# A two-layer hybrid attention block on one NeuronCore: one first h from alternating chunks, dot products respread, stream order changed

## The chip, the cores and the metric

The kernel runs on 1 core of one Trainium2 chip, as a single launch. The metric is device time in microseconds (us), the median of 3 runs. TensorE multiplies matrices (PE, its weight loads PEld), VectorE (DVE), ScalarE (ACT) and GpSimd (POOL) do the elementwise work, SyncE (SP) issues most of the transfers from memory. "span" is the time from the first to the last instruction of one profiled execution.

## The reference, cut to what matters

512 latent and 256 context tokens of width 1024 pass through two layers. Each layer is a mixer and an MLP, and each of these is preceded by an RMS norm whose result is shifted and scaled by a conditioning vector:

```
sh1, sc1, g1, sh2, sc2, g2 = split(silu(c) @ ada_w[i] + ada_b[i], 6)      # the same for c_ctx
h = rms_norm(x, norm_mix[i]) * (1 + sc1) + sh1                            # latent; context with its own vector
x = x + g1 * mixer(h)                                                     # layer 0: window + neighbourhood, layer 1: latent attention
x = x + g2 * square(relu(modulate(rms_norm(x, norm_mlp[i]), sh2, sc2) @ w1)) @ w2
```

Layer 0's mixer projects h once (units kva, qa01, qa23, kqb0 to kqb3 and vb0 to vb3), runs 16 heads of attention in pairs, and projects the result. Layer 1's mixer is a low-rank latent attention.

## The kernel before, in words

Activations lie with the 1024 features on partitions, in 8 tiles k of 128 x 768 tokens (512 latent, 256 context). Nearly every product is made in three passes of TensorE: an operand is split into a high part and a remainder (hh and hl for h, wh and wl for weights), and `mm3` and `mm3t` add hh*wh, hl*wh and hh*wl. Weights arrive as 512 KB tiles through three buffers (`Weights`, `raws`); `pump` splits a tile (copy to wh, subtraction to wl on DVE or POOL) when a planner's clock says that it is near.

**The first stage** (from L1922) is written out by hand. Sixteen chunks of 512 KB of the conditioning matrix `ada_w` (scale: e = 1, shift: e = 0; four chunks c of 256 columns, two halves each) are issued by SP, all scale chunks first, with 1 KB rows. `part(e, c)` multiplies a chunk pair by the conditioning vectors, ACT copies the row out, and `turn(e, c)` transposes it and forms two tiles' worth of `mod` and, for the scale, of `coef`. Squares of x are taken by ACT and added by DVE (`acc`), `stats` sums them on PE, `rsq` gives 1/rms per token (`box`).

h is formed twice. `scaled(k)` makes hh and hl of x * coef, without 1/rms and without shift (2 ACT and 2 DVE operations per k), and `step(k)` adds tile k's part of the kva projection from them (18 matmuls, six outputs `first` in six PSUM banks). `hat(k)` multiplies x by 1/rms on POOL, and `whole(k)` applies scale and shift (2 ACT), copies hh (DVE or ACT) and subtracts hl (DVE or POOL). The missing shift of kva is made up by `shift_w` (24 matmuls on the split shift) and `shift_p`, and 1/rms and shift enter as `first` is copied out at the head of `mixer0`, by 12 DVE operations.

**The mixers** (`mixer0` L985, `mixer1` L1351) are ordered by `weave` (L233) while the program is built. Streams (projections `gemms`, `preps`, `finishes`, `scores` for the two halves of a head pair, `values`, the output projection's early part) yield what they wait for. A model of the engines (`Clock.note`, L67) estimates when each could go on (a transfer counts as its bytes / 350e3 us behind the one before, plus 2.0: 3.5 us for 512 KB); the earliest goes next, nothing counts as earlier than 0.4 us after PE's modelled time, and among equals the first in the list wins. In `mixer0` one more stream, `ada_stream` (L564), forms 24 further steps of the conditioning: each loads 512 KB into one of the three weight buffers (at most two held at once, one left for weights) and does 8 small matmuls into PSUM bank 7. When it has ended, `lend` gives that bank to the ring M, which the other streams use with three banks till then. It is last in the list of `mixer0`.

**After mixer0** `Out.rest` (L1813) finishes the output projection, m = 0 to 7, and forms the operands of the MLP (`Fold.put`). The remaining conditioning vectors are dot products on DVE (`Dots`, L594): `tick` does the one whose 512 KB are there (two operations of 128x1024 for the first 24, one for the other 32) and loads the next. `rest` ticks at m = 0, 1, 2; `mlp` of layer 0 ticks at the end of every hidden tile f (`end`, L1858) and of every output tile m. The first 8 must be done before the gate of that MLP is used.

Of the kernel before, what the change touches and what calls it, by code (L numbers as in the profile page):

```python
# [10 lines left out]
F32 = mybir.dt.float32  # L11
# [15 lines left out]
class Clock:  # L27
# [39 lines left out]
    def note(self, eng, fn, args, kw):  # L67
# [5 lines left out]
        if eng == "pe":  # L73
# [159 lines left out]
def weave(clock, streams, always):  # L233
# [39 lines left out]
def hybrid_block(  # L273
# [5 lines left out]
    ada_w: bass.AP,  # L279
    ada_t: bass.AP,  # L280
# [702 lines left out]
    def mixer0(hh, hl, ap, oT, proj, first, box):  # L983
# [325 lines left out]
        add2 = PT.get("shift_p")  # L1309
        copy(add2.rearrange("p (s n) -> p s n", s=2), first[6])  # L1310
        for i in range(6):
            if i % 2 == 0:
                kva.r.append(RAW.get(f"ur_kva{i // 2}", [128, 2, 128]))
            y, add = box[0][:, i:i + 1], add2[:, (i // 4) * 256:(i // 4 + 1) * 256]
            for dst, c in ((kva.r[-1][:, i % 2, :], slice(0, 128)), (va[:, i, :], slice(128, 256))):
                dve.scalar_tensor_tensor(dst, first[i][:, c], y, add[:, c], op0=ALU.mult, op1=ALU.add)
        PT.put(add2)
# [14 lines left out]
        def spare():  # L1332
# [18 lines left out]
    def mixer1(fold, proj, M):  # L1351
# [393 lines left out]
        for i in range(8):  # L1745
# [21 lines left out]
    class Out:  # L1767
# [45 lines left out]
        def rest(self, M, xt, g, fold, dots=None):  # L1813
            for m in range(8):
# [12 lines left out]
                if dots and m < 3:  # L1827
                    dots.tick()
# [7 lines left out]
    def mlp(M, layer, fold, xt, g, tags, nxt, dots=None):  # L1836
# [4 lines left out]
        for c in range(4):  # L1841
# [16 lines left out]
            def end(t):  # L1858
# [13 lines left out]
                if dots:  # L1872
                    dots.tick()
# [17 lines left out]
            for f in rest:  # L1891
                t = begin(f)
                products(t, range(8))
                end(t)
            if c == 3:
                fold.free()
# [28 lines left out]

    first = [t for ring_ in (banks(0, 1, 2, 3, 4, 5),) for t in (ring_.get(f"g_kva{i}", [128, 256]) for i in range(6))]
    with tc.tile_pool(name="az", bufs=1) as az:
# [4 lines left out]
        azw = Ring(ck, az, [f"ar{i}" for i in range(2)], [128, 256])  # L1932
        for e in (1, 0):
            for c in range(4):
                for half in range(2):
                    raw = azr.get(f"ada_raw{e}{c}{half}", [128, 4, 256])
                    col = e * 1024 + c * 256
                    sp.dma_start(raw, ada_w[half * 512:(half + 1) * 512, col:col + 256].rearrange(
                        "(g p) n -> p g n", p=128))
                    raws[e, c, half] = raw  # L1940
                if e == 1 and c in (0, 2):
# [8 lines left out]
        bs = [az.tile([128, 8, 2], F32R, name=f"shift{i}") for i in range(2)]  # L1950
        rr = az.tile([128, NT], F32, name="rr")
        rows_, held, box, wt = {}, {}, [], []
# [22 lines left out]
        def turn(e, c):  # L1975
            row = rows_.pop((e, c))
            pt = held[e, c] = B.get(f"ada_pt{e}{c}", [128, 2, 128])
# [13 lines left out]
            else:  # L1991
                dve.tensor_copy(bs[0][:, k, :], dst)
                dve.tensor_tensor(bs[1][:, k, :], dst, bs[0][:, k, :].bitcast(F32), op=ALU.subtract)

        def scaled(k):
            for x, si, t0, n in parts_of(x_sb, k):
                act.activation(hh[:, k, t0:t0 + n], x, AF.Copy, scale=coef[:, k, si:si + 1])
            for x, si, t0, n in parts_of(x_sb, k):
                dve.scalar_tensor_tensor(hl[:, k, t0:t0 + n], x, coef[:, k, si:si + 1],
                                         hh[:, k, t0:t0 + n].bitcast(F32), op0=ALU.mult, op1=ALU.subtract)  # L2000

        def step(k, i0=0, i1=6):
            for i in range(i0, i1):
                ts = slice(i * 128, (i + 1) * 128)
                mm3t(first[i], (hh[:, k, ts], hl[:, k, ts]), w(k), k == 0, k == 7)

        def hat(k):
            pool.tensor_tensor(x_sb[:, k, :], x_sb[:, k, :], rr, op=ALU.mult)

        def whole(k):  # L2010
            for x, si, t0, n in parts_of(x_sb, k):
                act.activation(x, x, AF.Identity, scale=coef[:, k, si:si + 1], bias=shift[:, k, si:si + 1])
            if k in (7,):
                act.activation(hh[:, k, :], x_sb[:, k, :], AF.Copy)
            else:
                dve.tensor_copy(hh[:, k, :], x_sb[:, k, :])
            e = pool if k in (2, 5) else dve
            e.tensor_tensor(hl[:, k, :], x_sb[:, k, :], hh[:, k, :].bitcast(F32), op=ALU.subtract)

        acc = azq.get("nacc_a0")  # L2020
        for k in range(8):
            sq = acc if k == 0 else azq.get(f"nsq_a0{k}")
            act.activation(sq, x_sb[:, k, :], AF.Square)
            if k:
# [3 lines left out]
        warm(42)  # L2028
        part(1, 0, 3)
        warm(3)  # L2030
        turn(1, 0)
# [234 lines left out]
```

## Time and profile before

| | us |
|---|---|
| median of 3 runs (lowest, highest) | 1822.18 (1821.94, 1822.3) |
| the profiled execution's own time | 1821.22 |
| its span | 1819.4 |
| its mean granted TensorE clock, share of full speed | 0.972 |

A busy share says how long an engine had an instruction in it, not that it ran at its peak. The granted clock is 1.00 at 2.4 GHz and 0.50 at 1.2 GHz. An idle time in brackets stands ahead of the instruction that ended it, with what released it. Nearly all instructions carry line 131, that of the recording helper, so they are told apart by the tiles they write.

### The profile page before, as it was taken

The page shows a single profiled execution, that of the slowest core. Times are in us where ns is not written, and L with a number is a line of the kernel's source. Part 1 is how long each engine was busy: PE and PEld are TensorE (multiplying, and loading weights), DVE is VectorE, ACT ScalarE, POOL GpSimd, SP SyncE. Part 2 cuts the span into 40 slices and gives each one's busy share as a digit, 9 for nine tenths or more (in the row PEclk, how much of TensorE's full clock was granted, in tenths as well). Part 3 has the DMA queues.
Part 4 walks back from the last instruction along what each step waited for, and adds up shares of the span by engine and source line. Part 5 has one row for each costly group of instructions (what it writes and reads, how often), then busy time and mean ns, then how long its engine had stood idle before and what let it go on. Part 6 is the DMA issues. An engine that isn't in the chain of part 4 may idle for free. (4 is left out here: it accounts for less than half of the span.)

```text
span 1819.4 us, 27725 instructions
## 1 busy us (share of the span) xinstructions
PE 1724.1 (95%) x11288; PEld 1478.9 (81%) x11288; DVE 1032.5 (57%) x1922; ACT 663.8 (36%) x1421; POOL 477.8 (26%) x249
## 2 busy tenths in 40 slices
PE   7889999888998999999999998799999999999999
PEld 6778778766887888888888898667776798989897
DVE  6777777663747665434454747877865652323242
ACT  4434555442223223123123234455655242324241
POOL 3222211121224422333333322312110233232322
PEclk9989999999998999999999999899989999999999
DMA  9310121223422444343433221001000233333332
GB/s 296 90 59 24 47 65 61 71 93 95 162 69 93 162 128 128 126 129 116 136 121 115 70 60 48 25 1 35 24 12 1 64 102 101 94 93 93 93 93 81
DMA packets 55807, 158.21 MB, mean 87 GB/s; under 512 B 7777, under 2 KB 18401, under 8 KB 55553
## 3 DMA queue, kind: packets, MB, share of 16 engines
q1 hardware_dynamic: 54336, 154.96, 27.1%
q8 instruction: 89, 1.46, 0.3%
q10 hardware_dynamic: 1344, 1.49, 0.3%
q14 instruction: 38, 0.30, 0.1%
HBM read 154.32 MB, written 2.11 MB: 86 GB/s over the span
## 5 line engine op out<-in xcount | busy, mean ns | idle before, releaser
L131 PE MATMUL p<-hh_m,wh_w 128*128 128x258 f32 (+2 forms) x1024 | 317.9, 310 | 0.3 <-DVE fr_m L131 0.3
L131 PE MATMUL p<-hl_m,wh_w 128*128 128x258 f32 (+2 forms) x1024 | 317.9, 310 | 0.0
L131 PE MATMUL p<-hh_m,wl_w 128*128 128x258 f32 (+2 forms) x1024 | 317.7, 310 | 0.0
L131 ACT ACTIVATE wh_w<-raw_w 128x1024 fp32r<-128x1024 f32 x114 | 120.3, 1059 | 442.6 <-PE p L131 411.2
L131 PE MATMUL p<-uh,wl_w 128*128 128x512 f32 (+1 forms) x768 | 273.1, 356 | 3.9 <-POOL wl_w L131 3.9
L131 PE MATMUL p<-uh,wh_w 128*128 128x512 f32 (+1 forms) x768 | 273.3, 356 | 2.8 <-ACT wh_w L131 2.8
L131 PE MATMUL p<-ul,wh_w 128*128 128x512 f32 (+1 forms) x768 | 274.1, 357 | 0.0
L131 POOL TENSOR_TENSOR wl_w<-raw_w,wh_w 128x1024 fp32r<-128x1024 f32 x70 | 179.3, 2561 | 318.6 <-ACT wh_w L131 263.1
L131 PEld LDWEIGHTS p<-hh_m,wl_w 128*128 128x128 f32 x1024 | 193.4, 189 | 11.1
L131 PEld LDWEIGHTS p<-hh_m,wh_w 128*128 128x128 f32 x1024 | 192.9, 188 | 11.7 <-DVE fr_m L131 0.5
L131 PEld LDWEIGHTS p<-hl_m,wh_w 128*128 128x128 f32 x1024 | 193.1, 189 | 11.2
L131 DVE SCALAR_TENSOR_TENSOR x<-p,mod,x 128x512 f32<-128x512 f32 x96 | 60.3, 658 | 198.7 <-PE p L131 198.6
L131 PEld LDWEIGHTS p<-uh,wl_w 128*128 128x128 f32 x768 | 145.7, 190 | 25.7 <-POOL wl_w L131 4.5
L131 PEld LDWEIGHTS p<-uh,wh_w 128*128 128x128 f32 x768 | 145.9, 190 | 24.5 <-ACT wh_w L131 3.2
L131 POOL TENSOR_TENSOR ul<-u,uh 128x512 fp32r<-128x512 f32 (+1 forms) x52 | 95.9, 1845 | 261.3 <-DVE uh L131 261.3
L131 PEld LDWEIGHTS p<-ul,wh_w 128*128 128x128 f32 x768 | 145.7, 190 | 20.8
L131 DVE SCALAR_TENSOR_TENSOR dots<-dot_raw,dots 128x1024 f32<-128x1024 f32 x80 | 132.6, 1657 | 39.2 <-DMA dot_raw<-in_ada_t_dram 38.3
L131 DVE TENSOR_TENSOR wl_w<-raw_w,wh_w 128x1024 fp32r<-128x1024 f32 x58 | 91.8, 1583 | 100.5 <-ACT wh_w L131 100.2
L131 DVE CAST uh<-u 128x768 fp32r<-128x768 f32 (+1 forms) x64 | 35.9, 561 | 101.2 <-ACT u L131 101.2
L131 PEld LDWEIGHTS pp_c<-ident,P 128*128 128x128 f32 x384 | 45.4, 148 | 26.4 <-issue 14.5
L131 ACT ACTIVATE r<-r,bs_p 128x256 f32<-128x256 f32 x64 | 38.5, 613 | 70.9 <-DVE r L131 68.8
L131 PE MATMUL pp_c<-ident,P 128*128 128x128 f32 x384 | 56.8, 291 | 7.9 <-DVE kb L131 3.1
(505 smaller groups left out, 3540.9 us busy)
## 6 DMA issues: line engine op xcount, KB each, us to landing
raw_w<-in_mlp_w_dram SPq DMA_DIRECT2D x128, 512.0 KB, 3.6
dot_raw<-in_ada_t_dram SPq DMA_DIRECT2D x56, 512.0 KB, 3.6
ada_raw<-in_ada_w_dram SPq DMA_DIRECT2D x40, 512.0 KB, 5.2
raw_kqb<-in_e_w_in_dram SPq DMA_DIRECT2D x8, 512.0 KB, 3.7
raw_eo<-in_e_w_out_dram SPq DMA_DIRECT2D x8, 512.0 KB, 3.6
raw_oo<-in_o_w_out_dram SPq DMA_DIRECT2D x8, 512.0 KB, 3.4
raw_oi<-in_o_w_in_dram SPq DMA_DIRECT2D x6, 512.0 KB, 3.6
bt<-in_bias_dram SPq DMA_DIRECT2D x4, 640.0 KB, 4.7
```

Of the source, the lines that this page charges most:

```text
L131: r = f(*a, **k)
```

## The change

It touches four places. (1) The chunks of `ada_w` come from a second copy in memory laid out in rows of 4 KB, scale and shift in turn for each c; h is formed once, with 1/rms, scale and shift, before `step(k)` uses it; `hat` moves from POOL to DVE; `scaled`, `shift_w` and `shift_p` go; `first` takes three banks instead of six and is copied out as it is. DVE takes the square of tile 7. (2) `rest` ticks at m = 0 to 4, and the MLP's first two hidden tiles don't tick. (3) The planner's PE costs are multiplied by 0.95 and its floor of 0.4 us becomes 0.5. (4) The stream lists of both mixers are reordered; in `mixer0` the conditioning stream stands ahead of `gemms` and `early`, and `values` behind `scores` and `preps`.

```diff
 # Clock.note, eng == "pe"
+            cost *= 0.95
 # weave
-                est = max(est, clock.t["pe"] + 0.4)
+                est = max(est, clock.t["pe"] + 0.5)
 # mixer0: kva out of PSUM
-        add2 = PT.get("shift_p")
-        copy(add2.rearrange("p (s n) -> p s n", s=2), first[6])
-        for i in range(6):
...
-                dve.scalar_tensor_tensor(dst, first[i][:, c], y, add[:, c], op0=ALU.mult, op1=ALU.add)
+        for b in range(3):
+            r = RAW.get(f"ur_kva{b}", [128, 2, 128])
+            copy(r, first[b][:, :, 0:128])
+            copy(va[:, 2 * b:2 * b + 2, :], first[b][:, :, 128:256])
+            kva.r.append(r)
 # mixer0: streams behind masks, biases, spare, lend
-                   values(halves, M, O, P, PT, RB, SU),
                    scores(halves, S, P, SU, 0, turn),
                    scores(halves, S, P, SU, 1, turn),
+                   preps(jobs, M),
+                   values(halves, M, O, P, PT, RB, SU),
                    finishes(jobs, M),
-                   preps(jobs, M),
+                   chain(ada_stream(A, M, PT, [(1, 2), (2, 1)], 2), lend(A, M, 1, lambda: True)),
                    gemms(jobs[1:], M, end),
-                   proj.early(M, (0, 1), lambda: bool(end), finished, 1),
-                   chain(ada_stream(A, M, PT, [(1, 2), (2, 1)], 2), lend(A, M, 1, lambda: True))], W.pump)
+                   proj.early(M, (0, 1), lambda: bool(end), finished, 1)], W.pump)
 # mixer1: streams
                    values(halves, M, O, P, PT, RB, SU),
+                   scores(halves, S, P, SU, 1, turn),
+                   finishes(fins, M),
                    scores(halves, S, P, SU, 0, turn),
-                   finishes(fins, M),
                    preps(jobs, M),
-                   scores(halves, S, P, SU, 1, turn),
 # Out.rest, mlp.end
-                if dots and m < 3:
+                if dots and m < 5:
-                if dots:
+                if dots and (c or f > 1):
 # first stage
-        for e in (1, 0):
-            for c in range(4):
+        for c in range(4):
+            for e in (1, 0):
...
-                    sp.dma_start(raw, ada_w[half * 512:(half + 1) * 512, col:col + 256].rearrange(
-                        "(g p) n -> p g n", p=128))
+                    sp.dma_start(raw, ada_s[e, c, half].rearrange("p (g n) -> p g n", g=4))
-                if e == 1 and c in (0, 2):
+                if (c, e) in ((0, 1), (1, 0)):
                     W.load(1)
...
         def hat(k):
-            pool.tensor_tensor(x_sb[:, k, :], x_sb[:, k, :], rr, op=ALU.mult)
+            dve.tensor_tensor(x_sb[:, k, :], x_sb[:, k, :], rr, op=ALU.mult)
 
         def whole(k):
+            full = azq.get(f"h_a0{k}")
             for x, si, t0, n in parts_of(x_sb, k):
-                act.activation(x, x, AF.Identity, scale=coef[:, k, si:si + 1], bias=shift[:, k, si:si + 1])
...
-            e.tensor_tensor(hl[:, k, :], x_sb[:, k, :], hh[:, k, :].bitcast(F32), op=ALU.subtract)
+                act.activation(hh[:, k, t0:t0 + n], x, AF.Identity, scale=coef[:, k, si:si + 1],
+                               bias=shift[:, k, si:si + 1])
+                dve.tensor_scalar(full[:, t0:t0 + n], x, coef[:, k, si:si + 1], shift[:, k, si:si + 1],
+                                  op0=ALU.mult, op1=ALU.add)
+            dve.tensor_tensor(hl[:, k, :], full, hh[:, k, :].bitcast(F32), op=ALU.subtract)
...
+            if k == 7:
+                dve.tensor_tensor(sq, x_sb[:, k, :], x_sb[:, k, :], op=ALU.mult)
+                dve.tensor_tensor(acc, acc, last, op=ALU.add)
...
-        warm(42)
+        warm(46)
         part(1, 0, 3)
         warm(3)
-        turn(1, 0)
...
+        turn(1, 0)
         next(factor)
         run(factor)
+        part(0, 0, 3)
+        warm(6)
+        for e, (t0, n) in zip((act, dve), SEG):
+            r = B.get(f"nr_a0{t0}")
+            spread(r, box[0], t0, n)
...
+        turn(0, 0)
+        hat(0)
+        whole(0)
+        W.pump(True, dve)
         wt.append(W.take("kva_0"))
+        part(1, 1, 3)
+        hat(1)
+        whole(1)
+        warm(6)
+        part(0, 1, 3)
+        warm(6)
+        hat(2)
+        hat(3)
+        for c in range(4):
+            k = 2 * c
+            step(k)
+            if c < 3:
+                turn(1, c + 1)
+                turn(0, c + 1)
+                whole(k + 2)
+            if c == 0:
+                W.pump(True, dve)
+                wt.append(W.take("kva_1"))
+            if c < 2:
+                part(1, c + 2)
+            step(k + 1)
+            if c == 1:
+                W.release(wt[0])
+            if c < 3:
+                whole(k + 3)
+            if c < 2:
+                part(0, c + 2)
+                hat(k + 4)
+                hat(k + 5)
+            if c == 2:
+                W.pump(True, dve)
+        W.release(wt[1])
```

## Rows read from the trace of the kernel before

**Rows 1.** The stretches of the span, one row each: us, then busy time (and instructions) of PE, PEld, DVE, ACT and POOL, granted clock, DMA share, GB/s.
```profile
0.00:72.00 72.00, 56.04 (x468) 46.11 (x469) 54.52 (x88) 36.44 (x62) 24.75 (x16) 0.94 0.73 220
72.00:130.00 58.00, 50.17 (x347) 46.29 (x348) 41.05 (x101) 16.51 (x39) 12.70 (x10) 0.88 0.23 75
130.00:380.00 250.00, 236.34 (x1959) 197.87 (x1959) 167.74 (x413) 124.59 (x402) 42.64 (x27) 0.98 0.15 49
380.00:450.00 70.00, 57.59 (x415) 40.59 (x414) 37.93 (x80) 26.62 (x71) 12.21 (x7) 0.90 0.38 121
...
530.00:600.00 70.00, 63.30 (x340) 54.30 (x341) 52.95 (x63) 22.55 (x31) 34.56 (x15) 0.93 0.27 90
600.00:1070.00 470.00, 469.62 (x2699) 413.61 (x2698) 242.73 (x367) 118.37 (x153) 142.82 (x55) 1.00 0.39 121
...
1100.00:1425.00 325.00, 290.80 (x1920) 227.65 (x1919) 229.03 (x487) 166.37 (x438) 57.02 (x41) 0.94 0.06 18
```

**Rows 2.** TensorE in order of time around the end of the first stage: start us, us, engine, line, operation, out<-in, count, and the idle time ahead of it.
```profile
64.03 0.39 PE L131 MATMUL g_qa<-wh_qa,hh_a 128*128 128x256 f32 x1
...
71.77 0.58 PE L131 MATMUL g_qa<-wl_qa,hh_a 128*128 128x256 f32 x1 [5.39 <-DVE wl_qa L131]
...
77.43 0.28 PE L131 MATMUL g_qa<-wh_qa,hh_a 128*128 128x256 f32 x1
```

**Rows 3.** VectorE's groups in the first 75 us: busy us, mean ns of one, idle before.
```profile
L131 DVE TENSOR_TENSOR hl_a<-x_in,hh_a 128x768 fp32r<-128x768 f32 x6 | 9.2, 1554 | 0.2
...
L131 DVE TENSOR_TENSOR nacc_a<-nacc_a,nsq_a 128x768 f32<-128x768 f32 x7 | 6.7, 957 | 0.6
...
L131 DVE CAST hh_a<-x_in 128x768 fp32r<-128x768 f32 x7 | 3.8, 556 | 0.5 <-ACT x_in L131 0.5
...
L131 DVE TENSOR_REDUCE mc<-ada_pt 128x4 f32<-128x16 f32 x8 | 1.3, 164 | 0.1
L131 DVE TENSOR_TENSOR wl_kva<-raw_kva,wh_kva 128x1024 fp32r<-128x1024 f32 x1 | 1.2, 1212 | 0.0
```

**Rows 4.** VectorE in order of time in the first stage.
```profile
11.18 7.33 DVE L131 TENSOR_TENSOR nacc_a<-nacc_a,nsq_a 128x768 f32<-128x768 f32 x7
...
26.21 1.14 DVE L131 SCALAR_TENSOR_TENSOR hl_a<-x_in,coef_a,hh_a 128x512 fp32r<-128x512 f32 x2
...
71.63 0.34 DVE L131 SCALAR_TENSOR_TENSOR ur_kva<-g_kva,y_a,shift_p 128x128 f32<-128x128 f32 x1
```

**Rows 5.** The conditioning stream in mixer0: everything on its PSUM tile, and whom it waited for.
```profile
L131 PE MATMUL ada_ps<-ada_raw,sT x192: 379/379/637, 120.7 to 430.8; 128*32 128x256 f32 x192
...
  DMA ada_raw<-in_ada_w_dram: 21.4, 11
```

**Rows 6.** TensorE in the last part of mixer0: one step of the conditioning stream, 8 matmuls, at half clock.
```profile
393.39 1.08 PE L131 MATMUL ada_ps<-ada_raw,sT 128*32 128x256 f32 x8 [4.43 <-DMA ada_raw<-in_ada_w_dram]
```

**Rows 7.** VectorE in the output projection and in the first MLP's first hidden tiles.
```profile
492.99 1.14 DVE L131 SCALAR_TENSOR_TENSOR x<-ps_eo,mod,x 128x512 f32<-128x512 f32 x2 [0.96 <-PE ps_eo L131]
...
501.39 1.14 DVE L131 SCALAR_TENSOR_TENSOR x<-ps_eo,mod,x 128x512 f32<-128x512 f32 x2 [2.33 <-PE ps_eo L131]
...
517.32 0.69 DVE L131 CAST wh_w<-raw_w 128x1024 fp32r<-128x1024 f32 x1 [12.29 <-PE p L131]
...
533.31 1.22 DVE L131 SCALAR_TENSOR_TENSOR dots<-dot_raw,dots 128x1024 f32<-128x1024 f32 x1
...
544.82 1.01 DVE L131 TENSOR_TENSOR r<-p,fr_m 128x256 f32<-128x256 f32 x2
...
554.47 1.00 DVE L131 TENSOR_TENSOR r<-p,fr_m 128x256 f32<-128x256 f32 x2
...
560.82 3.30 DVE L131 SCALAR_TENSOR_TENSOR dots<-dot_raw,dots 128x1024 f32<-128x1024 f32 x1
```

**Rows 8.** TensorE's two waits in that MLP.
```profile
575.38 0.54 PE L131 MATMUL p<-uh,wh_w 128*128 128x512 f32 x1 [2.82 <-ACT wh_w L131]
...
580.21 0.79 PE L131 MATMUL p<-uh,wl_w 128*128 128x512 f32 x1 [3.86 <-POOL wl_w L131]
```

**Rows 9.** Two stretches around these waits, columns as in the first group.
```profile
575.00:580.00 5.00, 0.97 (x2) 0.30 (x2) 4.67 (x3) 0.33 (x1) 4.95 (x2) 0.57 0.00 0
580.00:585.00 5.00, 4.79 (x11) 3.80 (x12) 3.08 (x7) 3.02 (x4) 0.54 (x2) 0.50 0.50 187
```

**Rows 10.** TensorE in order of time: the sums of squares, the spread of 1/rms, and the first and the last of the 18 matmuls of `step(7)`.
```profile
18.56 1.50 PE L131 MATMUL nst_a<-ones,nacc_a 128*128 128x1 f32 x12
...
27.89 1.60 PE L131 MATMUL nr_a<-ident,y_a 128*128 128x128 f32 x12
...
57.41 0.28 PE L131 MATMUL g_kva<-wh_kva,hh_a 128*128 128x256 f32 x1
...
59.45 0.28 PE L131 MATMUL g_kva<-wh_kva,hl_a 128*128 128x256 f32 x1
```

**Rows 11.** ScalarE in order of time in the first stage.
```profile
55.42 1.30 ACT L131 ACTIVATE x_in<-x_in,mod,coef_a 128x512 f32<-128x512 f32 x2
```

**Rows 12.** SP's queue, issues of the chunks: start us, us; a row of several issues lasts till the last is out.
```profile
17.68 16.59 SPq L131 DMA_DIRECT2D ada_raw<-in_ada_w_dram  x10
```

**Rows 13.** The median time from issue to landing, in us, is the last column.
```profile
raw_w<-in_mlp_w_dram SPq DMA_DIRECT2D x128, 512.0 KB, 3.6
...
ada_raw<-in_ada_w_dram SPq DMA_DIRECT2D x40, 512.0 KB, 5.2
```

More of the change, by code (lines that the diff above doesn't have):

```diff
@@ L1923, in hybrid_block @@
     hl = big.tile([128, 8, NT], F32R, tag="B", name="hl_a0")
-    first = [t for ring_ in (banks(0, 1, 2, 3, 4, 5),) for t in (ring_.get(f"g_kva{i}", [128, 256]) for i in range(6))]
+    first = [ring_.get(f"g_kva{b}", [128, 2, 256]) for ring_ in (banks(0, 1, 2),) for b in range(3)]
     with tc.tile_pool(name="az", bufs=1) as az:
@@ L1990, in turn, with hat, whole @@
                     [128, 2, 2]), op0=ALU.add, op1=ALU.mult)
[L1991 to L1995, printed above, removed]
+        def hat(k):
+            dve.tensor_tensor(x_sb[:, k, :], x_sb[:, k, :], rr, op=ALU.mult)
+        def whole(k):
+            full = azq.get(f"h_a0{k}")
             for x, si, t0, n in parts_of(x_sb, k):
[L1997 to L2000, printed above, removed]
+                act.activation(hh[:, k, t0:t0 + n], x, AF.Identity, scale=coef[:, k, si:si + 1],
[3 more added lines that the diff above has]
+            dve.tensor_tensor(hl[:, k, :], full, hh[:, k, :].bitcast(F32), op=ALU.subtract)
+            azq.put(full)
         def step(k, i0=0, i1=6):
@@ L2038, in hybrid_block @@
         B.put(st)
-        part(1, 1, 3)
-        warm(6)
-        scaled(0)
+        turn(1, 0)
         next(factor)
         run(factor)
-        turn(1, 1)
-        scaled(1)
-        wt.append(W.take("kva_0"))
-        step(0)
-        part(1, 2)
-        scaled(2)
-        rs = [B.get(f"nr_a0{t0}") for t0, n in SEG[:1]]
-        spread(rs[0], box[0], *SEG[0])
-        act.activation(rr[:, 0:NL], rs[0], AF.Copy)
-        B.put(rs[0])
-        rs.append(B.get("nr_a01"))
-        spread(rs[1], box[0], *SEG[1])
@@ L2056, in hybrid_block @@
-        act.activation(rr[:, NL:NT], rs[1][:, 0:NCX], AF.Copy)
-        B.put(rs[1])
-        scaled(3)
-        hat(0)
-        hat(1)
-        step(1, 0, 3)
-        turn(1, 2)
-        step(1, 3, 6)
-        W.pump(True, dve)
-        wt.append(W.take("kva_1"))
-        scaled(4)
-        scaled(5)
-        step(2)
-        part(1, 3)
-        for k in range(2, 6):
-            hat(k)
-        step(3, 0, 3)
-        turn(1, 3)
-        step(3, 3, 6)
-        scaled(6)
-        part(0, 0)
-        scaled(7)
@@ L2078, in hybrid_block @@
-        hat(6)
-        hat(7)
-        step(4, 0, 3)
-        turn(0, 0)
-        part(0, 1)
-        step(4, 3, 6)
-        turn(0, 1)
-        part(0, 2)
-        whole(0)
-        step(5, 0, 3)
-        turn(0, 2)
-        whole(1)
-        step(5, 3, 6)
-        part(0, 3)
-        whole(2)
-        W.pump(True, dve)
-        step(6, 0, 3)
-        turn(0, 3)
-        whole(3)
-        step(6, 3, 6)
-        whole(4)
-        whole(5)
-        step(7)
-        ps = B.get("shift_w", [2, 256])
@@ L2102, in hybrid_block @@
-        for k in range(8):
-            mm3t(ps, (bs[0][:, k, :], bs[1][:, k, :]), w(k), k == 0, k == 7)
-        for x in wt:
-            W.release(x)
-        whole(6)
-        sw = azw.get("sw")
-        act.activation(sw[0:2, :], ps, AF.Copy)
-        B.put(ps)
-        first.append(pp.tile([128, 2, 256], F32, tag="b7", bufs=1, name="shift_p"))
-        for si in range(2):
-            mm(first[6][:, si, :], ident[0:2, si:si + 1].to_broadcast([2, 128]), sw[0:2, :], start=True, stop=True)
-        whole(7)
@@ L2127, in hybrid_block @@
     with tc.tile_pool(name="at0", bufs=1) as ap0:
[L2128 removed]
+        M0 = mixer0(hh, hl, ap0, oT, proj, first)
     late = ctx.enter_context(tc.tile_pool(name="late", bufs=1))
```

52 lines of the change are left out of this document (24 added, 28 removed).

## The prediction

> **What bounds the kernel now.** I read the stretches first: TensorE is busy nearly all the time, so time can be gained only where it stands or runs at the lower clock. It is full from 600 to 1070. It loses in four places [rows 1]: the first stage, mixer0, the first MLP's hidden tiles at 530 to 600, and mixer1 (34.2 us without PE work and a clock of 0.94).
>
> *First stage.* The projection proper (qa01) begins at 64.03, stands 5.39 us for VectorE's remainder of a weight tile, resumes at 71.77 and runs at about half speed till 77.43 [rows 2]. VectorE's 54.5 us of 72 [rows 1] is what it waits for: six subtractions of 128x768 took 1554 ns each, while the additions of the same size took 957 with POOL idle [rows 3]. It counts as begun at 72.7: 71.77, plus some 2.4 us for 26 matmuls at 0.21 instead of 0.12 us, less the 13 matmuls (1.5 us) done earlier. kva leaves PSUM in twelve operations from 71.63 on [rows 4].
>
> *mixer0.* From 72 to 450 PE has no work in 7.8 + 13.7 + 12.4 = 33.9 us, and clocks of 0.88, 0.98 and 0.90 cost about 7 + 5 + 7 us more [rows 1]. Of the standing, 21.4 us in 11 pieces are waits for the conditioning stream's transfers, which lasts from 120.7 to 430.8 [rows 5]; the longest, 4.43 us, stands in the tail of the mixer [rows 6].
>
> *First MLP.* Each hidden tile costs VectorE about 9.65 us (544.82 to 554.47 [rows 7]), of which two dot products are more than half; PE needs 8.4 for the same number and shapes of matmuls (VectorE's waits for it at 492.99 and 501.39 end that far apart [rows 7]). The lag grows until ScalarE's wh and POOL's wl of the first output weight come late: PE waits 2.82 and 3.86 us [rows 8] and runs at 0.57 and 0.50 of the clock [rows 9].
>
> **The change, part by part.**
>
> *A. The new first stage.* The additions end at 18.5 [rows 4]; VectorE's own square of tile 7 adds one operation of 1.05 us, so 19.6. The `stats` matmuls take 1.5 [rows 10]; then PE does `part(0, 0)` with its warming (my estimate 2.2), six more warm products and the spread of 1/rms (1.6 each [rows 10], twelve records both), and the copy out follows: 27.6. The four warm products added at the start end before the first chunk lands and cost nothing. From 27.6 VectorE has, in order:
> - 8 `hat` at 0.96 = 7.7 (price of the additions [rows 3], because nothing is left on POOL here)
> - 8 subtractions at 0.96 = 7.7
> - 8 pairs of `tensor_scalar` (512 and 256 columns). No row shows this form. The cast of 128x768 took 0.556 [rows 3], the three-operand pair 1.14 [rows 4]. I take 0.65, near the cast, since both read a single tensor: 5.2
> - 17 small operations of the remaining `turn`s at 0.2 = 3.4 [rows 3]
> - two weight remainders at 1.21 = 2.4 [rows 3]
> - waits for ScalarE: in five of the eight tiles hh starts only when `hat` or `coef` is done, and its pair lasts 1.30 [rows 11] + 0.1 against 0.65: 5 x 0.75 = 3.8
>
> Sum 30.2, so hl of tile 7 is there at 57.8. Beside that PE has tile 6 ready from about 56 and does two steps of 18 matmuls, 0.12 apart, 2.1 each [rows 10]: the last `step` ends at about 60.1. qa01's first remainder (1.2) lies beside it, the second on POOL or VectorE by 60.7, for matmuls not due before 61.5. The six plain copies of kva (about 1.4 us) replace 12 operations. Chunks don't set this: ten issues took 16.59 us [rows 12], the last was out at 34.3, and by 5.2 us to landing [rows 13] it is there by 40, while PE asks for it at 48. SP issues the same 16 chunks and the two kva tiles, in another order; the first kva tile still stands behind two chunks. Gone from PE: 24 `shift_w` matmuls (2.8) and `shift_p` (1.1), already beside VectorE's work. **72.7 to 60.1: 12.6 us.** With the pair at 1.14 only three tiles pay, as ScalarE covers the rest: 61.6, so 11.1. With the cast's price 12.9. Below, if PE stands longer at each `step` than counted, 6; above, if the small waits overlap, 16.
>
> *B. mixer0's order.* Now the 24 steps start at once, two buffers in turn, and POOL, VectorE and PE do projections between them. The planner counts 3.5 us for a transfer; the weights' median is 3.6, these chunks' 5.2 [rows 13]. I take 4.1, nearer the weights, whose loads also come one at a time: two in flight give a step every 2.05 us where it expects 1.75. That is 0.3, and 0.1 at the change of tile shape, per step: 24 x 0.4 = 10 of standing instead of 21.4 (with 3.6, 4; with 5.2, 23). Each step's PE work, half of 1.08 [rows 6] at full clock, only moves. Behind a waiting step stand all projections, on PE, and behind its load on SP the next weight tile, which the one remaining buffer lets run about 3 us late; a projection unit of two tiles lasts 34 us, so that hides. Where PE had nothing else, old steps filled time; I count 5 us lost to that, about half of their 13 us. Of the 19 us of clock loss, the pieces behind the long waits (3) come back. Bank 7 and the two buffers are free some 250 us earlier; no row prices that, and I count nothing for it, with up to 11 in the range. **11.4 + 3 - 5 = 9 us**, from 8 lost (nothing left to fill gaps, `values` delayed) to 20 gained.
>
> *C. Dots.* `rest` now does two dot products, at m = 3 and 4, and loads a third: two transfers move ahead of the MLP's weights on SP, 1.5 us each, with PE 12 us ahead. Their four operations of 1.22 to 3.30 us [rows 7] are 5 to 13 us on a VectorE that then waited 0.96, 2.33 and 12.29 us [rows 7]; what is over delays the last tile's operands, which PE first asks for after two hidden tiles' worth of other tiles, about 14 us. So that costs nothing; without that cover it would be 3. In the MLP the first two tiles lose about 4 us each, and VectorE's chain comes 8 us earlier. The waits of 2.82 + 3.86 go, and the clock's dip (some 13 matmuls at 0.43 instead of 0.23, 2.6 us): 9.3. Late next is hidden tile 6, whose remainder POOL finishes about 2 us after PE wants it. **7 us**, rounded down to 6.5; from 2 to 9.3.
>
> *D. Planner and mixer1.* PE costs at 0.95 and a floor of 0.5 change which stream wins; scores of the second half go up, those of the first down. The two alternate by their own rule, so only `finishes` and `preps` are passed. The 34 us of standing in mixer1 give it room both ways; no row gives a sign. **0**, from 8 lost to 8 gained.
>
> Sum: 12.6 + 9 + 6.5 = 28.1 off the profiled execution's 1821.2: 1793.1. The median of the runs shown is 1.0 above that execution, so 1794.
>
> **A rule against the change.** In the first stage PE stood 5.39 us and came back at the lower of the clock's two levels [rows 2]; after its two waits in the MLP the granted clock was 0.57 and 0.50 [rows 9]. The Trainium skill, "TensorE: Matmul & The Clock Gate", section "Why this matters for your kernels", says that idle gaps between bursts of matmuls put the engine back to its slow clock. The trace agrees on its own long gaps. Here it would make the new stage's bursts slow, since every `step` waits for VectorE; rival 2 is that case.
>
> **Rivals.**
> 1. *mixer0 gives nothing back*: the steps were cheap filler and attention's chain on VectorE sets the pace. For it: the tail after the last projection runs through small dependent products. Against it: waits on transfers are the largest single item. 1821.2 - 19.1 + 1 = 1803.
> 2. *The first stage runs at the lower clock*: my order leaves PE gaps of 1 to 3 us between steps, shorter than the one that dropped it. If the last four steps take twice as long, 4 x 2.1 = 8.4 us: 1802.5.
> 3. *The steps hold TensorE* (the other side): PE takes its queue in order, and now everything behind a step waits for its transfer. It decides if a step waits more than about 1.7 us: 24 x 1.7 = 41 = 21.4 + 19.1. With chunks landing in 5.2 us [rows 13] where the planner counts 3.5, a pair of steps waits up to 4.4: 12 x 4.4 = 53, 31 more than now, and no 3 of clock: 1821.2 - 19.1 + 31 + 1 = 1834.
> 4. *The freed bank and buffers pay*: 11 more in mixer0 and some in mixer1: 1779.
> 5. *The change of order does nothing*, because weights and buffers, not ranks, set who is ready: as rival 1, and counted there.
>
> **How the numbers follow.** Forecast 0.52; rival 1 0.17; rival 2 0.10; rival 3 0.10; rival 4 0.11. The likeliest is 1794. The range of 8 in 10 reaches from rival 4 to rival 1 and a loss of some us in mixer1 on top: 1776 to 1818. A measurement here can tell about 0.2%, 3.6 us, from no change. Faster by more: the forecast, rivals 2 and 4 and nearly all of rival 1: 0.85. Within it: where rival 1 meets losses in mixer1, 0.06. Slower: rival 3, less a part that ends between, 0.09.
>
> **What would show it.** qa01's first matmul at 58 to 62 without a wait over 2 us, at full clock, and the 128x768 operations of VectorE near 0.96 throughout. The conditioning stream over before about 140 us, its waits for transfers at 10 us or less. No waits of PE between 570 and 590 of the old time, the first dot products in the output projection. mixer1's length unchanged within 8 us. The forecast is wrong if PE waits for `ada_raw` more than 20 us, if the first stage's end moves by less than 6 us, or if mixer0's length grows.

## The result, and the profile after

The changed kernel takes 1797.8 us (median of 4 runs, 1795.1 to 1801.57) beside 1822.24 for the kernel before on the same chip: a ratio of 0.9866, with a 95% interval of 0.9845 to 0.9887, 24.4 us less. Its profiled execution lasted 1799.72 and had a span of 1797.9, 21.5 less than before. The forecast was 1794, and it counted 28.1 off the profiled execution. The total came out near; one of its three terms did not.

The work's milestones (first and last matmuls of the units' tiles in the two traces) cut the span into stages. Mixer0 is counted to the last product of the output projection, and its start in the kernel before is the effective 72.7 of the prediction. Counted from a common point instead, qa01's hundredth matmul (84.74 before, 70.92 after), the first stage gains the same 13.8, and mixer0 loses the same 0.4 (416.7 and 417.1 us from there).

| stage | before | after | gained | forecast |
|---|---|---|---|---|
| first stage, to qa01 | 72.7 | 58.9 | 13.8 | 12.6 |
| mixer0 and its output projection | 428.7 | 429.1 | -0.4 | 9 |
| first MLP, to mixer1's first projection | 551.0 | 540.9 | 10.1 | 6.5 |
| mixer1, to the last product of its output projection | 401.3 | 403.2 | -1.9 | 0 |
| second MLP, to the end of the span | 365.7 | 365.8 | -0.1 | 0 |

**First stage.** TensorE in order of time, after, where [rows 2] showed a stall of 5.39 us: start us, us, engine, line, operation, out<-in, shape, count.

```profile
58.80 0.28 PE L132 MATMUL g_kva<-wh_kva,hl_a 128*128 128x256 f32 x1
58.92 0.28 PE L132 MATMUL g_qa<-wh_qa,hh_a 128*128 128x256 f32 x1
59.05 0.28 PE L132 MATMUL g_qa<-wl_qa,hh_a 128*128 128x256 f32 x1
```

The projection follows kva's last matmul without a gap, and matmuls stand 0.12 apart. VectorE's groups of the first 75 us, forms apart (busy us, mean ns of one, idle before), answer to [rows 3]:

```profile
L132 DVE TENSOR_TENSOR hl_a<-h_a,hh_a 128x768 fp32r<-128x768 f32 x8 | 7.7, 958 | 2.7 <-ACT hh_a L132 2.4
L132 DVE TENSOR_TENSOR x_in<-x_in,rr 128x768 f32<-128x768 f32 x8 | 7.4, 951 | 0.0
...
L132 DVE TENSOR_SCALAR h_a<-x_in,coef_a,mod 128x512 f32<-128x512 f32 x8 | 4.4, 544 | 0.2
L132 DVE TENSOR_SCALAR h_a<-x_in,coef_a,mod 128x256 f32<-128x256 f32 x8 | 3.3, 407 | 0.0
```

The subtractions that took 1554 ns take 958, with POOL nearly idle beside them (2.33 us of work in the first 59, in the next row, against 24.75 in the first 72 before). The new form, a scale and a shift by one value per partition, costs 544 and 407 ns.

**Stretches.** After, the columns of [rows 1]:

```profile
0.00:59.00 59.00, 54.24 (x471) 46.11 (x472) 38.69 (x83) 24.84 (x40) 2.33 (x5) 1.00 0.76 246
59.00:130.00 71.00, 59.83 (x472) 48.23 (x471) 46.16 (x105) 26.55 (x71) 15.24 (x11) 0.93 0.43 141
130.00:176.00 46.00, 45.07 (x429) 33.64 (x428) 24.88 (x68) 19.78 (x69) 1.79 (x2) 1.00 0.47 154
176.00:380.00 204.00, 190.59 (x1536) 163.43 (x1534) 145.28 (x343) 100.06 (x306) 31.92 (x21) 0.97 0.12 37
380.00:440.00 60.00, 49.08 (x321) 40.47 (x320) 38.98 (x75) 26.62 (x72) 15.83 (x8) 0.91 0.09 27
...
515.00:590.00 75.00, 74.76 (x427) 65.33 (x426) 55.10 (x76) 26.23 (x35) 28.52 (x11) 1.00 0.34 106
```

In the MLP's first hidden tiles (the last row) TensorE now stands 0.24 us at full clock, where 530 to 600 before had 6.7 us of standing and a clock of 0.93. Between 59 and 440 TensorE has no work in 11.2 + 0.9 + 13.4 + 10.9 = 36.4 us; before it was 33.9. So mixer0 stands as long as it did, although the conditioning stream is over early and hardly waits. Everything on its tile, answering to [rows 5] (a view that counts most waits twice, as before_short shows below):

```profile
L132 PE MATMUL ada_ps<-ada_raw,sT x192: 379/379/636, 85.5 to 173.1; 128*32 128x256 f32 x192
...
  DMA ada_raw<-in_ada_w_dram: 4.8, 10
```

What stands in its place shows in TensorE's waits of mixer0, after (waiter, what it waited for: us in total, times, longest us), and in two rows of TensorE in order of time further down:

```profile
PE c_a L132 <- ACT P_a L132: 8.9, 3, 6.8
PE ut_kqb L132 <- DVE q_kqb L132: 7.7, 1, 7.7
PE vtp_vb L132 <- DVE q_qa L132: 3.9, 2, 3.3
PE g_vb L132 <- DVE kw_kva L132: 3.3, 1, 3.3
...
PE ada_ps L132 <- DMA ada_raw<-in_ada_w_dram: 1.9, 5, 0.8
```

The same view of the kernel before, from 72 to 502 (the two rows ahead of these are the waits for chunks, 9.8 us in 5, shown below under before_short, and the first stage's stall of 5.4):

```profile
...
PE g_vb L131 <- DVE kw_kva L131: 3.3, 1, 3.3
PE pp_bc L131 <- DVE k_kqb L131: 2.7, 1, 2.7
PE ps_eo L131 <- POOL ol L131: 2.3, 3, 1.2
```

And the two rows of TensorE after:

```profile
204.50 1.22 PE L132 MATMUL c_a<-kw_kva,q_qa 128*128 128x256 f32 x4 [6.75 <-ACT P_a L132]
...
395.64 0.66 PE L132 MATMUL ut_kqb<-ident,ur_kqb 128*128 128x128 f32 x2 [7.68 <-DVE q_kqb L132]
```

Two waits of attention on its own chains, 6.75 and 7.68 us, each longer than any wait for a chunk before; TensorE comes back from both at the lower clock, as the two stretches around them show (200 to 210: 0.50; 390 to 400: 0.56).

```profile
200.00:210.00 10.00, 5.50 (x25) 5.10 (x26) 8.47 (x14) 6.44 (x18) 2.36 (x1) 0.50 0.30 84
...
390.00:400.00 10.00, 4.36 (x20) 4.28 (x21) 8.90 (x12) 4.04 (x7) 2.46 (x1) 0.56 0.09 16
```

### The profile page after: what moved, and what is told of

It is laid out like the page before. It is cut to its first block, busy times and chain, and to the rows that moved or that the text cites. A ratio compares the mean times of both kernels' runs of the same rounds, so it can differ in the third digit from the quotient of the medians.

```text
span 1797.9 us, 27708 instructions
## 1 busy us (share of the span) xinstructions
PE 1720.0 (96%) x11304; PEld 1478.3 (82%) x11304; DVE 1034.4 (58%) x1907; ACT 663.0 (37%) x1417; POOL 441.9 (25%) x228
## 5 line engine op out<-in xcount | busy, mean ns | idle before, releaser
L132 POOL TENSOR_TENSOR wl_w<-raw_w,wh_w 128x1024 fp32r<-128x1024 f32 x64 | 163.2, 2550 | 310.3 <-ACT wh_w L132 265.3
L132 PEld LDWEIGHTS p<-hh_m,wh_w 128*128 128x128 f32 x1024 | 192.9, 188 | 11.6 <-ACT fr_m L132 0.4
L132 PEld LDWEIGHTS p<-hl_m,wh_w 128*128 128x128 f32 x1024 | 193.1, 189 | 11.2
L132 DVE SCALAR_TENSOR_TENSOR dots<-dot_raw,dots 128x1024 f32<-128x1024 f32 x80 | 147.2, 1840 | 40.6 <-DMA dot_raw<-in_ada_t_dram 39.4
L132 DVE SCALAR_TENSOR_TENSOR x<-p,mod,x 128x512 f32<-128x512 f32 x96 | 60.2, 658 | 188.6 <-PE p L132 188.6
L132 POOL TENSOR_TENSOR ul<-u,uh 128x512 fp32r<-128x512 f32 (+1 forms) x52 | 100.7, 1937 | 267.4 <-DVE uh L132 267.4
L132 DVE TENSOR_TENSOR wl_w<-raw_w,wh_w 128x1024 fp32r<-128x1024 f32 x64 | 97.6, 1525 | 115.1 <-ACT wh_w L132 108.2
L132 PE MATMUL l_c<-kb,D 96*128 96x512 f32 x192 | 62.0, 444 | 0.0
## 6 DMA issues: line engine op xcount, KB each, us to landing
ada_raw<-in_ada_s_dram SPq DMA_DIRECT2D x16, 512.0 KB, 10.2
```

Of the source, the lines that this page charges most:

```text
L132: r = f(*a, **k)
```

## The experiments

All were timed against the kernel before on their own chip, so ratios are compared; "us" below is the ratio times 1822.2. The stage lengths are from the profiles. Mixer0 runs here from qa01's first matmul as recorded; the old first stage's stall lies inside it, so the two halves of the table are not compared with each other.

| run | ratio (95% interval) | us | qa01 at | mixer0 | first MLP | mixer1 |
|---|---|---|---|---|---|---|
| *old first stage:* before | 1 | 1822.2 | 64.0 | 437.4 | 551.0 | 401.3 |
| b_alone | 1.0035 (1.0024 to 1.0047) | 1828.6 | 65.1 | 444.1 | 550.9 | 397.9 |
| c_alone | 0.9951 (0.9940 to 0.9963) | 1813.3 | 66.9 | 435.7 | 540.8 | 400.8 |
| d_alone | 0.9992 (0.9981 to 1.0004) | 1820.7 | 65.4 | 434.3 | 551.2 | 400.0 |
| before_short | 0.9976 (0.9967 to 0.9985) | 1817.8 | 67.2 | 432.5 | 551.0 | 401.3 |
| *new first stage:* after | 0.9866 (0.9845 to 0.9887) | 1797.8 | 58.9 | 429.1 | 540.9 | 403.2 |
| a_alone | 0.9957 (0.9946 to 0.9969) | 1814.4 | 61.5 | 433.2 | 551.1 | 401.4 |
| after_old_m0 | 0.9862 (0.9846 to 0.9878) | 1797.1 | 60.1 | 429.9 | 541.1 | 402.4 |
| after_ada_last | 0.9922 (0.9903 to 0.9941) | 1808.0 | 60.2 | 439.1 | 540.8 | 404.0 |
| after_values_first | 0.9911 (0.9897 to 0.9925) | 1806.0 | 59.9 | 436.1 | 541.1 | 401.3 |
| after_no_planner | 0.9913 (0.9899 to 0.9927) | 1806.3 | 60.3 | 436.4 | 540.9 | 403.6 |
| after_floor4 | 0.9926 (0.9905 to 0.9948) | 1808.7 | 57.7 | 441.3 | 540.7 | 398.0 |
| after_1k | 0.9880 (0.9861 to 0.9899) | 1800.3 | 59.0 | 429.1 | 541.2 | 403.2 |
| after_warm | 0.9883 (0.9870 to 0.9897) | 1800.9 | 58.9 | 429.1 | 541.0 | 402.9 |

The MLP's length has two values, set by the dot products alone. The three kernels with the changed kernel's order in mixer0 (after, after_1k, after_warm: the same 3024 matmuls in the same order) have 429.1 three times: its length belongs to the order. Before and c_alone share an order too and lie 1.2 us apart from qa01's hundredth matmul on (416.7 and 415.5). The start of qa01 moves with the clock in the first stage (last section), by up to 3.8 us with the same code ahead of it.

**The four parts, each by itself in the kernel before.**

The first stage alone (old lists, planner and dots):

> The kernel before with the new first stage alone (alternating chunks in 4 KB rows, one h, the square on VectorE, kva copied out of three banks). As predicted: 12.6 us off, 1809.6. As the trace of after reads (the first matmul of qa01 counts as begun at 72.7 before and at 58.9 after): 13.8 off, 1808.4. The rival that an earlier start only meets later waits of mixer0, so that its gain is partly given back: 1812 to 1820. Mixer0 from qa01's first matmul to the end of the output projection then 435 to 440 us long instead of 428.5.

7.8 us off. The start came 11.2 us earlier than the effective 72.7, not 13.8: this execution ran at half clock while 1/rms was made (last section). Mixer0, with its old list, took 433.2 from there, 4.5 more than 428.7. The time lies where it was expected if an earlier start is partly given back, but mixer0 is shorter than the 435 to 440 expected with it. The planner also ordered this mixer0 otherwise than the kernel before's, so it is not shown whether the earlier start or the other order cost the 4.5.

Mixer0's list alone:

```diff
-                   values(halves, M, O, P, PT, RB, SU),
                    scores(halves, S, P, SU, 0, turn),
                    scores(halves, S, P, SU, 1, turn),
+                   preps(jobs, M),
+                   values(halves, M, O, P, PT, RB, SU),
                    finishes(jobs, M),
-                   preps(jobs, M),
+                   chain(ada_stream(A, M, PT, [(1, 2), (2, 1)], 2), lend(A, M, 1, lambda: True)),
                    gemms(jobs[1:], M, end),
-                   proj.early(M, (0, 1), lambda: bool(end), finished, 1),
-                   chain(ada_stream(A, M, PT, [(1, 2), (2, 1)], 2), lend(A, M, 1, lambda: True))], W.pump)
+                   proj.early(M, (0, 1), lambda: bool(end), finished, 1)], W.pump)
```

> The kernel before with mixer0's new stream list alone, the conditioning stream ahead of the projections and values behind scores. As predicted: 9 us off, 1813. As the two traces read (mixer0 428.5 us long before, 428.9 after, from qa01's first matmul to the last product of the output projection): nothing, 1822, within 3 us; PE's waits for the conditioning chunks under 10 us and its waits for ScalarE and VectorE inside attention longer by about as much as was saved. If the steps hold TensorE: over 1826.

6.4 us slower: the number given for steps that hold TensorE, from another cause. The conditioning steps waited 1.0 us; attention waited in their place: from qa01's hundredth matmul on, TensorE's other waits are 37.6 us against 24.0 in the kernel before. What the lower clock cost there, taken as (1 - mean granted clock) x length, is 22.2 against 17.1 us. The waits of TensorE in its mixer0:

```profile
PE ut_kqb L131 <- DVE q_kqb L131: 7.7, 1, 7.7
PE c_a L131 <- DVE q_qa L131: 6.1, 2, 4.8
...
PE c_b L131 <- DVE q_kqb L131: 4.3, 1, 4.3
...
PE ada_ps L131 <- DMA ada_raw<-in_ada_w_dram: 1.0, 2, 0.7
```

The dots alone (`m < 5` in `rest`, `c or f > 1` in `end`):

> The kernel before with the dot products respread alone. As predicted: 6.5 us off, 1815.7, with about 2 us left at hidden tile 6. As the trace of after reads (from the last product of the output projection to mixer1's first projection: 551.2 us before, 541.1 after): 10 off, 1812, and no wait of PE over 1 us in the MLP. If the waits only went because everything upstream moved, under 4 off: over 1818.

8.9 us off, the MLP at 540.8. TensorE's only wait from 503 to 1040:

```profile
PE p L131 <- DVE fr_m L131: 0.3, 1, 0.3
```

Planner numbers and mixer1's list:

> The kernel before with the planner's factor 0.95 and floor 0.5 and with mixer1's new stream list, and with mixer0's old list. As predicted: 0, 1822, within 8 us either way. As the two traces read (from mixer1's first projection to the last product of its output projection 400.6 us before, 402.5 after): 2 us slower in mixer1, 1824, and mixer0, whose order the planner also sets, changed by an amount that neither theory gives.

1.5 us, not told apart from nothing. The four add up to 7.8 - 6.4 + 8.9 + 1.5 = 11.8 off, and together they gave 24.4. The MLP's gain is the same everywhere, so most of the other 12.6 us is interplay in mixer0 and mixer1; up to 2.6 of it can be a_alone's later start. By the intervals the 12.6 is good to some 6 us. The next runs come at it from the other end, undoing pieces in the changed kernel.

**Pieces undone in the changed kernel.** Mixer0's whole list as before:

> The changed kernel with mixer0's stream list as before (conditioning stream last, values first), all else changed. As predicted (the list is worth 9 us): 1807. If the list alone costs the 7 us that it cost in the kernel before: 1791. If its worth depends on what stands around it (first stage, planner), so that the shortfall of the parts run singly against the whole, about 12 us, lies in this pair: 1803 or more.

The same time: the list that cost 6.4 in the kernel before is worth nothing that can be told here (0.7 dearer). Neither the predicted 9 nor an additive 7 held. By these sums 5.7 of the 12.6 us of interplay are the list's (6.4 less 0.7). The other 6.9 lie among the rest: first stage, dots and planner with mixer1's list take 7.8 + 8.9 + 1.5 = 18.2 off singly and 25.1 together in this run. Each of these figures is good to a few us. Bank 7 was freed at about 412 in this run and at 173 in the changed kernel, with mixer0 within 0.8 us.

Half of the list, the conditioning stream last and `values` still late:

> The changed kernel with the conditioning stream alone back at the end of mixer0's list; values stay behind scores and preps. As predicted, 8 of the 9 us come from this rank: 1806. If the rank is worth nothing because attention's own waits take the place of the transfers': 1798, within 3 us, with PE's waits for the chunks back at 10 to 20 us and its waits for ScalarE and VectorE shorter by about as much. If it costs time: 1791 to 1795.

10.2 us slower on the common scale. Taken alone that looks like the predicted worth of the rank. TensorE's waits for chunks in mixer0 are 11.8 us in 7 here against 1.9, 9.9 more, and the sum of its other waits there is 29.3 us against 34.2: 5 of the 9.9 are given back. So 5 of mixer0's 10 us are standing; the rest lies in the clock, which over the same stretch was 0.948 against 0.963, a cost of 22.2 against 15.4 us.

The other half, `values` first and the conditioning stream ahead of the projections:

> The changed kernel with values alone back at the head of mixer0's list, the conditioning stream still ahead of the projections. The whole list undone gave 1797.6 and the conditioning stream alone put last 1809.9, so values behind scores cost 12 there with the stream last. If the two halves of the list add up, values first is worth the same 12 here: 1786, faster than both kernels. If an order's worth is not a sum of its parts: 1793 to 1805, and mixer0 426 to 437 us from qa01's first matmul to the last product of the output projection.

8.2 us slower, 1 above the second range; mixer0, at 436, is in its. So each half undone costs 8 to 10, both undone cost nothing: the worth of a rank depends on the other ranks.

The planner's factor and floor as before, and then the floor alone:

> The changed kernel with the planner's PE costs and floor as before (factor 1, floor 0.4), both new lists and all else kept. As predicted: no change, 1798, within 8. If the new list of mixer0 pays only with the new planner numbers: 1804 or more, and mixer0 longer than 428.9 us from qa01's first matmul to the last product of the output projection, with mixer1 changed by less than 3 us.

8.5 us slower, of which mixer0's length has 7.3: numbers that alone were worth nothing that can be told are worth 8.5 beside the new first stage and lists. The signs of the second theory are there, but its reason is not the whole: by after_old_m0, the old list does as well with the new numbers.

> The changed kernel with the planner's floor back at 0.4 us and its factor 0.95 kept; the whole planner undone gave 1807.3. If the two numbers steer the order smoothly: between 1798 and 1807. If any other number gives another order and with it another mixer0, without a rule: anywhere from 1794 to 1812, mixer0 427 to 440 us from qa01's first matmul to the last product of the output projection, while the first MLP stays at 541 and the second at 366.

With 0.4 instead of 0.5 us and the factor kept: 10.9 slower, no less than with both undone. Mixer0 took 441.3, above its range and the longest with the new first stage, and mixer1 398.0, one of the shortest. Four neighbours of the changed kernel (two list halves, two planner settings) gave mixer0 436 to 441, two orders gave 429 to 430. No rule that orders these settings was found in the traces.

**What a wait for a chunk is worth.** The order on TensorE is that of the kernel before; only the transfers are shorter, while the planner still counts 512 KB:

```diff
-        sp.dma_start(raw, ada_w[k * 128:(k + 1) * 128, c:c + 1024].rearrange("p (g c) -> p g c", g=4))
+        src = ada_w[k * 128:(k + 1) * 128, c:c + 1024].rearrange("p (g c) -> p g c", g=4)
+        sp.eng.dma_start(raw[:, 0:1, :], src[:, 0:1, :])
+        ck.note("dma", "dma_start", (raw, src), {})
...
-            mm(ps[32 * g:32 * g + 32, e * 256:(e + 1) * 256], sT[:, k, :], raw[:, g, :],
+            mm(ps[32 * g:32 * g + 32, e * 256:(e + 1) * 256], sT[:, k, :], raw[:, 0, :],
```

> The kernel before with an unchanged order on every engine, but each of the 24 transfers of mixer0's conditioning stream brings only its first quarter (128 KB instead of 512), and the step multiplies that quarter four times; so the conditioning vectors of layer 0 are other ones. It takes away most of the waits for transfers and nothing else. As predicted (waits for chunks are TensorE's largest loss in mixer0, and 11 to 14 us come back with them, clock included): 1808 to 1811. If attention's chain on ScalarE and VectorE takes their place: 1817 to 1822, with PE's waits for the chunks under 5 us and its other waits in mixer0 longer.

4.4 us off (2.7 to 6.0 by the interval). It lies in the range of the second theory, and that one's signs are there: chunk waits under 5 us, other waits longer. But the run's first finding was in reading the kernel before again, through TensorE's own waits and those of its weight loads:

```profile
PE ada_ps L131 <- DMA ada_raw<-in_ada_w_dram: 9.8, 5, 4.4
...
PEld ada_ps L131 <- DMA ada_raw<-in_ada_w_dram: 11.6, 6, 4.9
```

9.8 + 11.6 is the 21.4 in 11 pieces of [rows 5]: the view by tile adds the idle time of the weight load and that of the matmul, and these are the same stretches of time (4.91 and 4.43 us end at 393.38 and 393.39). TensorE stood 9.8 us for chunks, not 21.4. With short transfers:

```profile
PE pp_ac L131 <- DVE k_kqb L131: 3.3, 2, 1.8
...
PE ada_ps L131 <- DMA ada_raw<-in_ada_w_dram: 2.9, 2, 2.4
```

6.9 us of these waits went, and mixer0 got 437.4 - 432.5 = 4.9 shorter, 4.3 from qa01's hundredth matmul on. There TensorE's other waits grew from 24.0 to 27.7 us (pp_ac waited 1.8 for the same tile before), so 3.2 of the 6.9 stayed as less standing; the rest of the gain is clock, which cost 15.4 us instead of 17.1.

**Two details of the first stage.** The chunks in rows of 1 KB, as before:

> The changed kernel with the first stage's chunks read from the old copy, in rows of 1 KB instead of 4 KB; order and all else kept. As predicted (the chunks don't set the first stage): no change, 1798, within 2 us, with the last chunk some us later and no new wait of TensorE for a chunk. If the rate matters: 1800 to 1803, with a wait for ada_raw ahead of the third or fourth chunk pair and qa01's first matmul later by as much.

1800.3 is 2.5 above the changed kernel, just outside the 2 given, but the other theory's wait for ada_raw isn't there: stage by stage the lengths are the changed kernel's, and the ratios' intervals overlap. The rate did change, as the stretch from 18 to 27 of after_1k and of the changed kernel shows (last column, GB/s), and nothing waited over 0.3 us for it.

```profile
18.00:27.00 9.00, 7.41 (x71) 5.71 (x70) 3.06 (x13) 1.40 (x4) 0.00 (x0) 1.00 1.09 357
```

```profile
18.00:27.00 9.00, 8.70 (x81) 6.49 (x77) 2.89 (x13) 1.78 (x5) 0.00 (x0) 1.00 1.02 408
```

Nine more warm products ahead of the sums of squares (`warm(3)` to `warm(12)`), the order of all else kept:

> The changed kernel with twelve instead of three warm products between the first chunk's products and the sums of squares; the order of everything else is the same. In four of the five profiles of the new first stage so far TensorE stood 0.71 to 1.11 us there, then ran at half clock for 3 to 7 us, and qa01 began at 60.1 to 61.5; in the fifth it didn't stand and qa01 began at 58.9. If that standing is what drops the clock: full clock from 18 to 30, qa01's first matmul at 58.5 to 60, and the time 1796 to 1797 with less scatter than 1795 to 1801. If the clock falls for another reason: the dip stays in the profile, and the added 0.96 us makes it 1798 to 1799.

Full clock in its profile and qa01 at 58.9; the four runs lie within 1.8 us (1799.53 to 1801.28) where the changed kernel's lay within 6.5. The time, above both ranges, is not told apart from the changed kernel's, so no faster version came of it.

## Why the prediction was right, and where it was wrong

**A, the first stage: right, 13.8 for 12.6.** 1/rms was on VectorE at 26.25 instead of 27.6, because the sums of squares began at 19.09 instead of 19.6 and what stands between them and the copied 1/rms took 0.8 less than estimated. The 0.8 is nearly all in the copy out: the prediction's terms add up to 26.5 and leave 1.1 for it, and VectorE's part took 0.42. From there to the last hl the sum was 30.2 and the trace has 30.3 (56.54), with two terms off against each other: the `tensor_scalar` pair 0.87 us instead of 0.65 (1.7 more over eight), the waits for ScalarE 2.4 instead of 3.8. The `step` after it took the 2.4 us that were counted. That the chunks' rate doesn't set this stage, after_1k bears out. The two profiles compared both lack a dip of the clock; over all of them qa01's hundredth matmul comes at 85.8 on average with the old stage (five profiles, 84.7 to 87.3) and at 71.6 with the new (nine, 69.7 to 73.5), 14.1 earlier.

**B, mixer0: wrong, nothing for 9.** The 9 was 11.4 + 3 - 5. From qa01's hundredth matmul to the last product of the output projection the two traces have these terms: waits for chunks 9.8 before and 1.9 after, so 7.9 gained for 11.4; cost of the clock 17.1 and 15.4, so 1.7 for 3; and all other waits of TensorE 24.0 and 34.2, so 10.2 lost for 5. The sum is -0.6, beside a measured -0.4. The step that failed most is therefore "I count 5 us lost to that": attention's own waits took back twice as much, all that was gained.

The first term rests on a misreading, "Of the standing, 21.4 us in 11 pieces are waits for the conditioning stream's transfers", which counted each wait nearly twice, on the weight load and on the matmul; the size was 9.8. The 10 that was to stay was too high as well (1.9), which hid most of that error. Two of the prediction's own signs spoke against B: the stream was to be over before about 140 us and lasted to 173.1, and mixer0's length, which was not to grow, grew by 0.4. With the order held, 6.9 us less of such waits gave 4.4; with the order changed, 7.9 less gave nothing.

Rival 1 (chance 0.17) is what mixer0 did, and its reason fits: the waits that grew are nearly all for VectorE and ScalarE, as the lists of waits show. By 173 the filler is used up, and at 204.5 and 395.6 TensorE found nothing else to do. That the steps' earlier place brought this about is read from the two traces, not isolated: after_old_m0, with the steps last, has a mixer0 of the same length. That the total came out near is luck in part: B's 9 missing us stand against 1.2 in A and 3.6 in C, mixer1 lost 1.9, and the medians differ by 2.9 more than the two profiled executions.

**C, the dots: right, under-sized, 10.1 for 6.5.** The two waits and the dip went, 9.3. What was subtracted for hidden tile 6 ("POOL finishes about 2 us after PE wants it") never came: no wait over 0.3 us is left in the MLP. Cover for the dots in the output projection was there too: the first two ran at 466.5 and 474.9, and VectorE's last operand of the MLP ends at 490.65, 2.4 us after the last product.

**D, planner and mixer1: 0 by itself, but not a term of a sum.** mixer1 lost 1.9, which can't be put down to its list, because with the same list and planner numbers in d_alone it was 1.3 shorter. The planner's numbers, alone not told apart from nothing, are worth 8.5 in the changed kernel through mixer0, which the prediction had put under B. "0, from 8 lost to 8 gained" held where D stood alone and missed its place in the sum.

**Rivals.** 2 (lower clock): not in the profiled execution, which has 1.00 from 0 to 59. Five of nine profiles of the new stage have a stretch at half clock, not between the steps but where 1/rms is made, and qa01 then begins at 59.9 to 61.5 instead of 57.7 to 59.0: 1 to 3 us, not 8.4. The gaps between the steps, expected at 1 to 3 us, were 0.93 us at the longest in the changed kernel. The Trainium skill ("TensorE: Matmul & The Clock Gate", "Why this matters for your kernels") has idle gaps between bursts of matmuls put the engine back to its slow clock. The trace agrees at the two long waits of mixer0 (6.75 and 7.68 us, followed by 0.50 and 0.56). 3 (steps hold TensorE): no; they waited 1.9 us in 5 pieces, 0.8 at the longest, and mixer0's 24 chunks landed in a median of 3.8 us; the 5.2 of [rows 13] was a median over both stages' chunks. The list did cost 6.4 in the kernel before, but through attention's waits. 4 (freed bank and buffers): nothing of it shows, as after_old_m0 frees the bank at 412 instead of 173 and has a mixer0 only 0.8 longer, though in another order. 5 (the change of order does nothing) fits the list in the changed kernel and not the list in the kernel before.

**Open.** Why just these settings of list and planner give mixer0 429 and their neighbours 436 to 441 is not settled. It is shown that the length belongs to the order and that the parts don't add; which early decision makes the difference was not isolated. What the four neighbours lose against the changed kernel can be read: 1.9 to 4.8 us more standing of TensorE and 1.7 to 8.5 us more at the lower clock.

## What to carry to other kernels

A view that groups by tile adds the waits of weight loads and of matmuls; before a wait becomes a term of a sum, look it up among the waits of the engine whose time it is. In a stretch where attention's dependent products and filler share TensorE, a wait removed was worth less than its length (4.4 us for 6.9 with the order held), because other waits grew; its worth is found with the order held still, and the clock is counted beside the waits. Where a planner sets the order, the worth of a rank or of a planner's number measured alone says little of its worth beside other changes: list such parts together, with one range, and undo them in the final kernel before believing either sign.

## What was not expected of the hardware

The clock's dip while 1/rms is made comes and goes with the same code, in the old stage too: before has 1.00 from 18 to 27, and b_alone, c_alone, d_alone and before_short, whose first stage is the same, have 0.81, 0.67, 0.81 and 0.67. Neither before nor c_alone stood directly ahead of the sums of squares. The stretch in before and in c_alone:

```profile
18.00:27.00 9.00, 8.08 (x73) 6.61 (x76) 5.98 (x16) 3.53 (x8) 2.35 (x1) 1.00 1.09 357
18.00:27.00 9.00, 8.09 (x51) 6.28 (x51) 4.89 (x11) 3.59 (x8) 2.35 (x1) 0.67 1.09 357
```

In the new stage, execution of a_alone, TensorE in order of time, and its stretch from 18 to 27:

```profile
16.81 0.94 PE L131 MATMUL warm<-ident 128*128 128x128 f32 x6
18.86 1.88 PE L131 MATMUL nst_a<-ones,nacc_a 128*128 128x1 f32 x12 [1.11 <-DVE nacc_a L131]
```

```profile
18.00:27.00 9.00, 8.14 (x48) 6.00 (x49) 1.96 (x9) 0.80 (x3) 0.00 (x0) 0.62 1.03 410
```

It stood 1.11 us and then ran at 0.62 of the clock in this stretch. after_1k stood 1.35 us at the same place, and its row above has 1.00. A stand of 0.32 us (after_values_first) was followed by 0.81. So the stand alone doesn't decide; what else does stays open. The one profile with products filling that place (after_warm) has no dip, which a single profile can't prove.

From 18 to 27 the transfers in 4 KB rows came at 408 GB/s and those in 1 KB rows at 357, with the DMA engines busy throughout in both (shares 1.02 and 1.09).
